# A two-layer hybrid encoder on one core: key blocks of the attention weights transposed two at a time instead of one at a time

## The chip, the core and the metric

The kernel runs on one NeuronCore of a Trainium2 chip, in a single launch. The metric is the device time of that launch in microseconds. A core has a matrix engine (TensorE, PE in the profile, with its weight loads as PEld), VectorE (DVE), ScalarE (ACT), GpSimd (POOL) and SyncE (SP, which here only issues transfers). Each engine works through its own list of instructions in order. They meet through semaphores, and the matrix engine writes only to PSUM, which DVE and ACT then read.

## The reference

Two layers, each with three attention branches side by side (MLA, a windowed GQA called SWA, and a differential attention), a gate on each, and an output product. The change touches the last step of two of the branches, the product of the attention weights with the values:

```python
# MLA, 8 heads, 512 tokens
p = jax.nn.softmax(s, axis=-1).astype(v.dtype)
return jnp.einsum('bhqk,bkhd->bqhd', p, v)
# differential attention, 4 heads
p = jax.nn.softmax(s, axis=-1)
a = p[:, 0] - lam * p[:, 1]
return jnp.einsum('bhqk,bkhe->bqhe', a.astype(v.dtype), v)
```

All is float32. The kernel holds accuracy by splitting a float32 operand in a rounded high part and the remainder, and multiplying high by high, low by high and high by low.

## The kernel before

Activations lie transposed, features on partitions and the 512 tokens along the free dimension. Large projections (`proj_T`, line 464) load a 128x1024 piece of weights into a tile `wr` (two buffers), ACT makes the high part `wh` (`act_copy`, L81), DVE the low part `wl` (`sub`, L84), and PE runs 24 products of 128x512 into a PSUM tile `ps_dn` (two buffers; `mm3`, lines 87 to 89).

An attention head has two steps. `first` makes the scores into `ps_sc` (two buffers), DVE takes the row maxima (L770), ACT the exponentials, and POOL scales the rows (L775), which leaves the weights `p` with queries on partitions. `second` needs keys on partitions. So for each block of 128 keys, `transposed_block` (line 701) takes a PSUM tile `ps_tr` (two buffers), has PE transpose four 128x128 pieces into it (L704), and copies it out in two parts: ACT writes the high part `pt` (L81), then DVE the low part, another `pt` (L84; `pt` has six buffers). Then PE multiplies both parts with the values into `ps_av` (one buffer): `av_step` in MLA (lines 713 to 717, two products a block), `mm3` in the differential attention (three a block). There are four blocks a head. After the last block the sum is read out of `ps_av` (L788 in MLA), and only then can the next head use that buffer.

`pipelined` (line 694) writes `first` of head h+1 before `second` of head h. SWA has a `second` of its own (line 898), which the change doesn't touch, but which uses the same `ps_tr`, `pt` and `ps_av`.

The written order is not the order on the engines. The kernel is handed to a scheduler, which goes through a model of the time, gives each tile a buffer when one is free, and puts each engine's instructions in the order in which they become ready there, with the written order as priority. So the loops mix: projections for later steps fill PE between the pieces of a head. `mod_late` (line 239) shares this stretch of layer 0: it loads pieces of `w_ada` into `wr` and sums them on DVE (L248, L251), and adds the result up through a `ps_dn` tile (L257, read by L261).

Of the kernel before, what the change touches and what calls it, by code (L numbers as in the profile page):

```python
# [17 lines left out]
P = 128  # L18
# [3 lines left out]
NT = S // P  # L22
# [28 lines left out]
def hybrid_kernel(ctx, tc, x, c, w_ada, b_ada, g_pre, g_post, w_in, g_q, w_uq, g_kv, w_ukv,  # L51
# [11 lines left out]
    def T(tag, shape, dt=F32, bufs=None):  # L63
        count[0] += 1
        return sb.tile(shape, dt, tag=tag, name=f"{tag}_{count[0]}",
                       bufs=bufs or BUFS.get(tag, 1))
# [6 lines left out]
    def Q(tag):  # L73
        count[0] += 1
        return ps.tile([P, S], F32, tag=tag, name=f"ps_{tag}_{count[0]}", bufs=PB[tag])

    def f(ap):
        return ap.bitcast(F32)

    def act_copy(out_, in_, scale=1.0):  # L80
        return act.activation(out=out_, in_=in_, func=AF.Copy, scale=scale)  # L81

    def sub(out_, a, b, eng=None):
        return (eng or dve).tensor_tensor(out=out_, in0=a, in1=b, op=ALU.subtract)  # L84

    def mm3(o, ah, al, bh, bl, start, stop):
        pe.matmul(o, ah, bh, start=start, stop=False)  # L87
        pe.matmul(o, ah, bl, start=False, stop=False)  # L88
        pe.matmul(o, al, bh, start=False, stop=stop)  # L89
# [392 lines left out]
    def split_u(o):  # L482
        uh = T("u", [P, S], F32R)
        ul = T("u", [P, S], F32R)
        act_copy(uh, o)
        sub(ul, o, f(uh))
        return uh, ul
# [213 lines left out]
    def transposed_block(blocks):  # L701
        tr = Q("tr")
        for i, b in enumerate(blocks):
            pe.transpose(tr[:, i * P:(i + 1) * P], b, ident)  # L704
        ph = T("pt", [P, S], F32R)
        pl = T("pt", [P, S], F32R)
        act_copy(ph, tr)
        sub(pl, tr, f(ph))
        return ph, pl

    def av_step(av, v, ph, pl, first, last):
        if not last:
            pe.matmul(av, v, ph, start=first, stop=False)  # L713
            pe.matmul(av[0:64], v[:, 0:64], pl, start=False, stop=False)  # L714
        else:
            pe.matmul(av[0:64], v[:, 0:64], pl, start=False, stop=False)
            pe.matmul(av, v, ph, start=False, stop=True)

    def mla_attention(l, cl, kp, v, wts):
# [59 lines left out]
        def second(h, pr):  # L779
            i = h % 2  # L780
            op = o_all[h // 2]
            av = Q("av")
            for kb in range(NT):
                ph, pl = transposed_block([pr[:, t, kb * P:(kb + 1) * P] for t in range(NT)])
                av_step(av, v[kb][:, h], ph, pl, kb == 0, kb == NT - 1)
            ol = T("ta", [P, S])
            act_copy(ol[0:64], av[64:128])
            dve.tensor_tensor(out=op[i * 64:(i + 1) * 64], in0=av[0:64], in1=ol[0:64], op=ALU.add)  # L788

        weights(0)  # L790
        prep(0)
        pipelined(first, second, 8)
        return o_all

# [142 lines left out]
    def diff_attention(l, hh, hl, fill):  # L937
# [31 lines left out]
        def second(hd, pr):  # L969
            vt = ops[hd][3]  # L970
            av = Q("av")
            for kb in range(NT):
                ph, pl = transposed_block([pr[:, t, kb * P:(kb + 1) * P] for t in range(NT)])
                vs = slice(kb * P, (kb + 1) * P)
                mm3(av, vt[:, 0, vs], vt[:, 1, vs], ph, pl, kb == 0, kb == NT - 1)
            sq = T("ta", [P, S])
            sqh = T("pt", [P, S], F32R)
            sql = T("pt", [P, S], F32R)
            act.activation(out=sq, in_=av, func=AF.Square)
            act_copy(sqh, sq)  # L980
            sub(sql, sq, f(sqh))
            sq_ps = Q("pj")
            pe.matmul(sq_ps, onesr, sqh, start=True, stop=False)
            pe.matmul(sq_ps, onesr, sql, start=False, stop=True)
            rs = T("ta", [P, S])
            act.activation(out=rs, in_=sq_ps, func=AF.Ln, scale=1.0 / P, bias=epsc)
            act.activation(out=rs, in_=rs, func=AF.Exp, scale=-0.5)
            o = T("o", [P, S])
            dve.scalar_tensor_tensor(out=o, in0=av, scalar=gsub[l], in1=rs, op0=ALU.mult,
                                     op1=ALU.mult)  # L990
            dve.tensor_tensor(out=o, in0=o, in1=zc[hd], op=ALU.mult)
            o_all.append(split_u(o))
# [4 lines left out]
        with tc.high_priority(offset=20):  # L997
            pr = first(0)
        for hd in range(4):
            zc[hd] = silu_z(l, C_ZC + hd * P, hh, hl)  # L1000
            fill(FN)
            if hd + 1 < 4:
                with tc.high_priority(offset=20):
                    nxt = first(hd + 1)
            with tc.high_priority(offset=20):
                second(hd, pr)
            pr = nxt
            if hd + 2 < 4:
                ops[hd + 2] = diff_qkv(l, hd + 2, hh, hl)
# [210 lines left out]
```

## Time and profile before

| | us |
|---|---|
| median of 3 runs | 1179.66 (1179.07 to 1180.35) |
| profiled execution, its own time | 1178.78 |
| its span | 1176.7 |
| PE busy | 1146.0 (97%) |
| DVE busy | 844.2 (72%) |
| ACT busy | 631.5 (54%) |

Read it so: the span is from the first to the last instruction of the program, the execution's own time has what lies around it, 2.1 us. A busy share is an average over the whole span, so the table says which engine is closest to its limit, and the rows further down say where it waits. Matmuls are pipelined, so the busy time of one (about 0.39 us) is longer than the step from one start to the next.

### The profile page before, as it was taken

To read this page: it belongs to the slowest core of one execution; us is meant where nothing else is said; L and a number is where in the kernel's file an instruction comes from. 1 tells how busy PE (TensorE), PEld (TensorE's weight loads), DVE (VectorE), ACT (ScalarE), POOL (GpSimd) and SP (SyncE) were. 2 spreads that over 40 slices of the span, in tenths; PEclk is the share of its full clock that TensorE was granted. 3 is DMA by queue.
4 is the path that set the end of the run, shared out by engine and by line. 5 is a ranking of instruction groups with operands and counts; after the bars stand their busy time and mean duration, and the time that the engine had idled before them with its cause. 6 is when DMAs were issued, how large, how long until landed. Compare 5 with 4: busy or idle time off the path is not lost.

```text
span 1176.7 us, 15536 instructions
## 1 busy us (share of the span) xinstructions
PE 1146.0 (97%) x5428; PEld 946.0 (80%) x5428; DVE 844.2 (72%) x1754; ACT 631.5 (54%) x1250; POOL 181.3 (15%) x226
## 2 busy tenths in 40 slices
PE   5899999999999999999999999999999999999997
PEld 4768788878887888888888888888888888888886
DVE  7956686898866687876577567688786568786654
ACT  5355464655543457664357456565564346675432
POOL 4310212122210010101211011222121001100120
PEclk9899999999999999999999999999999999999999
DMA  9537532256355433433454432324533333334442
GB/s 340 190 92 217 186 106 76 72 145 186 108 141 164 110 81 87 117 107 126 143 184 135 114 108 75 86 52 123 157 97 92 95 95 96 88 99 115 136 159 92
DMA packets 169522, 146.86 MB, mean 125 GB/s; under 512 B 7679, under 2 KB 146999, under 8 KB 169444
## 3 DMA queue, kind: packets, MB, share of 16 engines
q1 hardware_dynamic: 166148, 140.08, 40.9%
q10 hardware_dynamic: 3168, 5.77, 1.3%
q8 instruction: 43, 0.70, 0.2%
q14 instruction: 35, 0.29, 0.1%
q0 software_dynamic: 128, 0.01, 0.0%
HBM read 135.83 MB, written 14.20 MB: 127 GB/s over the span
## 4 chain that ended last, share of the span: by engine, by line
PE 84%; DVE 6%; DMA 3%; issue 3%; ACT 1%; POOL 1%; SPq 0%; DVEq 0%; POOLq 0%; ACTq 0%
PE ps_dn L87 20%; PE ps_dn L89 20%; PE ps_dn L88 19%; PE ps_tr L704 5%; PE ps_sc L89 2%; PE ps_sc L87 2%; PE ps_sc L88 2%; PE ps_av L714 1%; PE ps_av L713 1%; PE ps_sc L952 1%; PE ps_sc L953 1%; DMA wr<-in_w_in 1%; DVE o L206 1%; PE ps_pj L87 1%; PE ps_pj L88 1%
## 5 line engine op out<-in xcount | busy, mean ns | idle before, releaser
L87 PE MATMUL ps_dn<-hTh,wh 128*128 128x512 f32 x840 | 331.8, 395 | 1.4 <-DVE zz L479 0.8
L89 PE MATMUL ps_dn<-hTh,wl 128*128 128x512 f32 x840 | 330.5, 393 | 0.4 <-DVE wl L84 0.4
L88 PE MATMUL ps_dn<-hTl,wh 128*128 128x512 f32 x840 | 330.1, 393 | 0.0
L84 DVE TENSOR_TENSOR wl<-wr,wh 128x1024 fp32r<-128x1024 f32 x141 | 178.9, 1269 | 98.5 <-ACT wh L81 97.5
L81 ACT ACTIVATE wh<-wr 128x1024 fp32r<-128x1024 f32 x141 | 149.1, 1058 | 162.7 <-PE ps_dn L88 111.2
L87 PEld LDWEIGHTS ps_dn<-hTh,wh 128*128 128x128 f32 x840 | 158.2, 188 | 33.2 <-PE ps_dn L89 1.0
L89 PEld LDWEIGHTS ps_dn<-hTh,wl 128*128 128x128 f32 x840 | 158.0, 188 | 33.3 <-DVE wl L84 0.9
L88 PEld LDWEIGHTS ps_dn<-hTl,wh 128*128 128x128 f32 x840 | 158.1, 188 | 31.7
L84 DVE TENSOR_TENSOR pt<-ps_tr,pt 128x512 fp32r<-128x512 f32 x136 | 92.2, 684 | 30.5 <-ACT pt L81 29.6
L81 ACT ACTIVATE pt<-ps_tr 128x512 fp32r<-128x512 f32 x136 | 78.8, 596 | 64.8 <-PE ps_tr L704 63.6
L775 POOL TENSOR_SCALAR p<-p,st 128x512 f32<-128x512 f32 x64 | 52.2, 834 | 279.3 <-DVE st L773 243.7
L704 PE MATMUL ps_tr<-ident,p 128*128 128x128 f32 x544 | 92.4, 273 | 0.9 <-POOL p L775 0.6
L704 PEld LDWEIGHTS ps_tr<-ident,p 128*128 128x128 f32 x544 | 69.5, 141 | 20.2 <-POOL p L775 1.8
L87 PE MATMUL ps_dn<-u,wh 128*128 128x512 f32 x192 | 75.9, 395 | 0.0
L89 PE MATMUL ps_dn<-u,wl 128*128 128x512 f32 x192 | 75.9, 395 | 0.0
L88 PE MATMUL ps_dn<-u,wh 128*128 128x512 f32 x192 | 75.2, 391 | 0.0
L963 POOL TENSOR_SCALAR ta<-ta,st 128x512 f32<-128x512 f32 x32 | 26.7, 834 | 306.9 <-ACT wh L81 143.1
L894 POOL TENSOR_SCALAR p<-p,st 128x256 f32<-128x256 f32 (+1 forms) x64 | 42.1, 676 | 157.7 <-DVE st L892 130.4
L771 ACT ACTIVATE p<-ps_sc,st 128x512 f32<-128x512 f32 x64 | 43.7, 685 | 28.0 <-DVE st L770 27.7
L770 DVE TENSOR_REDUCE st<-ps_sc 128x1 f32<-128x512 f32 x64 | 43.4, 686 | 21.3 <-PE ps_sc L89 20.8
L886 ACT ACTIVATE p<-p,st 128x256 f32<-128x256 f32 (+1 forms) x64 | 35.7, 558 | 21.9 <-DVE st L884 21.2
L959 ACT ACTIVATE p<-p,st 128x512 f32<-128x512 f32 x32 | 23.1, 723 | 38.8 <-DVE st L957 38.7
(345 smaller groups left out, 2100.5 us busy)
## 6 DMA issues: line engine op xcount, KB each, us to landing
wr<-in_w_in SPq DMA_DIRECT2D x105, 512.0 KB, 3.7
wr<-in_w_ada SPq DMA_DIRECT2D x32, 512.0 KB, 3.6
wr<-in_w_out SPq DMA_DIRECT2D x16, 512.0 KB, 3.6
big<-in_w_ada SPq DMA_DIRECT2D x10, 512.0 KB, 7.6
big<-in_x SPq DMA_DIRECT2D x8, 512.0 KB, 5.3
wr<-in_w_o_mla SPq DMA_DIRECT2D x8, 512.0 KB, 4.0
wr<-in_w_o_swa SPq DMA_DIRECT2D x8, 512.0 KB, 3.4
wr<-in_w_o_diff SPq DMA_DIRECT2D x8, 512.0 KB, 3.7
```

The lines of the kernel that those rows point to most:

```text
L81: return act.activation(out=out_, in_=in_, func=AF.Copy, scale=scale)
L84: return (eng or dve).tensor_tensor(out=out_, in0=a, in1=b, op=ALU.subtract)
L87: pe.matmul(o, ah, bh, start=start, stop=False)
L88: pe.matmul(o, ah, bl, start=False, stop=False)
L89: pe.matmul(o, al, bh, start=False, stop=stop)
L704: pe.transpose(tr[:, i * P:(i + 1) * P], b, ident)
L770: dve.tensor_reduce(out=nm[:, t:t + 1], in_=s, axis=AX.X, op=ALU.max, negate=True)
L771: act.activation(out=pr[:, t], in_=s, func=AF.Exp, bias=nm[:, t:t + 1], accum_out=sm[:, t:t + 1])
L775: pool.tensor_scalar(out=pr[:, t], in0=pr[:, t], scalar1=rr[:, t:t + 1], scalar2=1.0, op0=ALU.mult, op1=ALU.mult)
L886: act.activation(out=pr[:, i, :w], in_=pr[:, i, :w], func=AF.Exp, bias=nm[:, i:i + 1], accum_out=sm[:, i:i + 1])
L894: pool.tensor_scalar(out=pr[:, i, :w], in0=pr[:, i, :w], scalar1=rr[:, i:i + 1], scalar2=1.0, op0=ALU.mult, op1=ALU.mult)
L963: pool.tensor_scalar(out=pc[1], in0=pc[1], scalar1=rr[:, 1:2], scalar2=1.0, op0=ALU.mult, op1=ALU.mult)
```

## The change

In both loops over the key blocks, the two blocks of a pair are now transposed and copied out in the written order before the products of either. No instruction is added or removed, and the products keep their order among themselves.

```diff
-            for kb in range(NT):
-                ph, pl = transposed_block([pr[:, t, kb * P:(kb + 1) * P] for t in range(NT)])
-                av_step(av, v[kb][:, h], ph, pl, kb == 0, kb == NT - 1)
+            for k0 in range(0, NT, 2):
+                pt = [transposed_block([pr[:, t, kb * P:(kb + 1) * P] for t in range(NT)])
+                      for kb in (k0, k0 + 1)]
+                for kb in (k0, k0 + 1):
+                    av_step(av, v[kb][:, h], *pt[kb - k0], kb == 0, kb == NT - 1)
```

The other loop, in the differential attention, is changed in the same way, with `mm3` in the place of `av_step`. Lines after the first loop stand two further down in the changed kernel (L788 becomes L790, L878 becomes L880), and names of tiles carry other numbers.

What the scheduler makes of it differs by place. In MLA of layer 1 no instruction moves on any engine. In the differential attention of either layer single transposes move by a few places. In layer 0, the lists start to differ in the fourth head of MLA and differ on through SWA, up to the first projections after it. In all, the transposes of L704 stand on PE in 196 uninterrupted rows before and in 188 now, of which rows of eight are 6 before and 11 now.

PE, layer 0, where the last MLA head's products start (`ps_av_1719`) beside the first scores of SWA (`ps_sc_25..`, L878). Before:

```order
L704 MATMUL ps_tr_1731<-ident_73,p_1638 128x128 x4
L257 MATMUL ps_dn_2440<-ones_78,u_2004 128x1 x4
L704 MATMUL ps_tr_1742<-ident_73,p_1638 128x128 x4
L878 MATMUL ps_sc_2515<-op_2202,op_2326 128x256
L879 MATMUL ps_sc_2515<-op_2203,op_2326 128x256
L878 MATMUL ps_sc_2535<-op_2202,op_2288 128x384
L879 MATMUL ps_sc_2535<-op_2203,op_2288 128x384
L713 MATMUL ps_av_1719<-pt_1725,big_866 128x512
L714 MATMUL ps_av_1719<-pt_1726,big_866 64x512
L713 MATMUL ps_av_1719<-pt_1736,big_873 128x512
L714 MATMUL ps_av_1719<-pt_1737,big_873 64x512
L704 MATMUL ps_tr_1753<-ident_73,p_1638 128x128 x4
```

The same place now (L880 is L878 of before, `pt_1734` and `pt_1735` are `pt_1736` and `pt_1737`):

```order
L880 MATMUL ps_sc_2515<-op_2202,op_2326 128x256
L881 MATMUL ps_sc_2515<-op_2203,op_2326 128x256
L257 MATMUL ps_dn_2440<-ones_78,u_2004 128x1 x4
L713 MATMUL ps_av_1719<-pt_1725,big_866 128x512
L714 MATMUL ps_av_1719<-pt_1726,big_866 64x512
L713 MATMUL ps_av_1719<-pt_1734,big_873 128x512
L704 MATMUL ps_tr_1742<-ident_73,p_1638 128x128 x4
L714 MATMUL ps_av_1719<-pt_1735,big_873 64x512
L704 MATMUL ps_tr_1751<-ident_73,p_1638 128x128 x4
L880 MATMUL ps_sc_2535<-op_2202,op_2288 128x384
L881 MATMUL ps_sc_2535<-op_2203,op_2288 128x384
L880 MATMUL ps_sc_2541<-op_2202,op_2289 128x384
```

The products into `ps_av_1719` moved ahead of the third block's transposes and of the second window's scores, and the first window's fourth score ahead of both.

DVE at the same place. Before (`ps_sc_2503` to `ps_sc_2515` are scores two to four of the first window, `o_1556` is the read-out of the head before):

```order
L248 TENSOR_SCALAR big_3119<-wr_3120,cact_66 128x512
L251 SCALAR_TENSOR_TENSOR big_3119<-wr_3120,cact_66,big_3119 128x512
L880 ISA p_2496,st_2491<-ps_sc_2503,x_548_2483,sinkt_72 128x256
L880 ISA st_2491 128x1
L880 ISA p_2496,st_2491<-ps_sc_2509,x_549_2486,sinkt_72 128x256
L880 ISA st_2491 128x1
L807 SCALAR_TENSOR_TENSOR op_2399<-ps_dn_2407,op_2399 64x512
L884 TENSOR_SCALAR st_2493<-st_2491 128x1
L788 TENSOR_TENSOR o_1556<-ps_av_1671,ta_1716 64x512
L884 TENSOR_SCALAR st_2493<-st_2491 128x1
L84 TENSOR_TENSOR pt_1737<-ps_tr_1731,pt_1736 128x512
L261 TENSOR_TENSOR ashf_8_70<-ps_dn_2440,prT_25_112 128x4
```

Now:

```order
L809 SCALAR_TENSOR_TENSOR op_2363<-ps_dn_2370,op_2363 64x512
L790 TENSOR_TENSOR o_1556<-ps_av_1671,ta_1716 64x512
L248 TENSOR_SCALAR big_3119<-wr_3120,cact_66 128x512
L84 TENSOR_TENSOR pt_1726<-ps_tr_1720,pt_1725 128x512
L84 TENSOR_TENSOR pt_1735<-ps_tr_1729,pt_1734 128x512
L251 SCALAR_TENSOR_TENSOR big_3119<-wr_3120,cact_66,big_3119 128x512
L882 ISA p_2496,st_2491<-ps_sc_2509,x_549_2486,sinkt_72 128x256
L882 ISA st_2491 128x1
L882 ISA p_2496,st_2491<-ps_sc_2515,x_549_2486,sinkt_72 128x256
L882 ISA st_2491 128x1
L809 SCALAR_TENSOR_TENSOR op_2399<-ps_dn_2407,op_2399 64x512
L261 TENSOR_TENSOR ashf_8_70<-ps_dn_2440,prT_25_112 128x4
```

The read-out of the head before and the two low parts `pt` of a pair stand together ahead of the scores of SWA, which they followed.

PE in SWA of layer 0, around one window's two transposed blocks (`ps_tr_2933`, `ps_tr_2944`) that no line of the diff touches. Before:

```order
L704 MATMUL ps_tr_2933<-ident_73,p_2832 128x128
L704 MATMUL ps_tr_2944<-ident_73,p_2832 128x128
L88 MATMUL ps_dn_3443<-hTl_121,wh_3438 128x512
L704 MATMUL ps_tr_2933<-ident_73,p_2832 128x128
L704 MATMUL ps_tr_2944<-ident_73,p_2832 128x128
L878 MATMUL ps_sc_2912<-op_2204,op_2399 128x384
L879 MATMUL ps_sc_2912<-op_2205,op_2399 128x384
L704 MATMUL ps_tr_2933<-ident_73,p_2832 128x128
L878 MATMUL ps_sc_2918<-op_2204,op_2400 128x384
L879 MATMUL ps_sc_2918<-op_2205,op_2400 128x384
L704 MATMUL ps_tr_2944<-ident_73,p_2832 128x128
L89 MATMUL ps_dn_3443<-hTh_120,wl_3439 128x512
```

Now, with the first products that use the blocks:

```order
L704 MATMUL ps_tr_2933<-ident_73,p_2832 128x128 x3
L704 MATMUL ps_tr_2944<-ident_73,p_2832 128x128
L704 MATMUL ps_tr_2933<-ident_73,p_2832 128x128
L704 MATMUL ps_tr_2944<-ident_73,p_2832 128x128 x3
L89 MATMUL ps_dn_3470<-u_2479,wl_3414 128x512
L257 MATMUL ps_dn_3484<-ones_78,big_3265 128x1 x4
L880 MATMUL ps_sc_2978<-op_2204,op_2362 128x256
L881 MATMUL ps_sc_2978<-op_2205,op_2362 128x256
L880 MATMUL ps_sc_2984<-op_2204,op_2363 128x256
L881 MATMUL ps_sc_2984<-op_2205,op_2363 128x256
L713 MATMUL ps_av_2932<-pt_2938,big_2245 128x512
L714 MATMUL ps_av_2932<-pt_2939,big_2245 64x512
```

The eight transposes moved into one row, behind two projections that they stood among, and nine products (one of 512 columns, four of one, four of 256) are left between them and the first product that needs them.

## Rows read from the trace of the kernel before

**Rows 1.** The page, part 1: busy us, share of the span, instructions.

```profile
PE 1146.0 (97%) x5428; PEld 946.0 (80%) x5428; DVE 844.2 (72%) x1754; ACT 631.5 (54%) x1250; POOL 181.3 (15%) x226
```

**Rows 2.** The page, part 4: the chain that ended last, by engine.

```profile
PE 84%; DVE 6%; DMA 3%; issue 3%; ACT 1%; POOL 1%; SPq 0%; DVEq 0%; POOLq 0%; ACTq 0%
```

**Rows 3.** Stretches: busy us of PE, PEld, DVE, ACT, POOL (instructions), granted clock, DMA.

```profile
190.00:245.00 55.00, 55.00 (x281) 44.79 (x280) 46.68 (x73) 32.16 (x64) 10.49 (x12) 1.00 0.30 87
245.00:253.00 8.00, 5.86 (x23) 4.23 (x23) 7.69 (x20) 4.57 (x11) 0.00 (x0) 0.79 0.58 138
253.00:380.00 127.00, 127.00 (x630) 105.83 (x630) 96.34 (x230) 63.19 (x132) 20.89 (x32) 1.00 0.52 147
...
700.00:870.00 170.00, 170.00 (x850) 139.85 (x849) 133.86 (x261) 102.28 (x216) 35.49 (x49) 1.00 0.35 98
```

**Rows 4.** Waits of PE, 125 to 1160 us: us in total, times, longest.

```profile
PE ps_sc L878 <- DVE st L880: 1.1, 1, 1.1
PE ps_av L713 <- DVE st L884: 0.9, 1, 0.9
PE ps_dn L87 <- DVE op L807: 0.6, 1, 0.6
PE ps_tr L704 <- POOL p L775: 0.6, 2, 0.3
```

**Rows 5.** Three short stretches, columns as in Rows 3.

```profile
140.00:150.00 10.00, 10.00 (x53) 8.23 (x52) 5.60 (x9) 4.83 (x12) 2.70 (x4) 1.00 0.27 80
245.00:249.00 4.00, 1.94 (x11) 1.19 (x10) 3.79 (x11) 1.01 (x3) 0.00 (x0) 1.00 0.81 177
249.00:253.00 4.00, 3.92 (x12) 3.03 (x13) 3.91 (x11) 3.57 (x9) 0.00 (x0) 0.57 0.36 99
```

**Rows 6.** PE in order of time: start us, busy us, line, tiles, [idle before].

```profile
149.32 1.03 PE L704 MATMUL ps_tr<-ident,p 128*128 128x128 f32 x8
150.11 0.48 PE L88 MATMUL ps_dn<-hTl,wh 128*128 128x512 f32 x1
150.42 0.40 PE L89 MATMUL ps_dn<-hTh,wl 128*128 128x512 f32 x1
150.65 0.39 PE L87 MATMUL ps_dn<-hTh,wh 128*128 128x512 f32 x1
...
157.01 0.60 PE L704 MATMUL ps_tr<-ident,p 128*128 128x128 f32 x4
157.37 0.48 PE L713 MATMUL ps_av<-pt,big 128*128 128x512 f32 x1
157.69 0.39 PE L89 MATMUL ps_dn<-hTh,wl 128*128 128x512 f32 x1
```

**Rows 7.** DVE in order of time, layer 0, end of MLA.

```profile
243.40 1.23 DVE L84 TENSOR_TENSOR wl<-wr,wh 128x1024 fp32r<-128x1024 f32 x1
...
247.57 0.68 DVE L807 SCALAR_TENSOR_TENSOR op<-ps_dn,op 64x512 fp32r<-64x512 f32 x1
...
248.36 0.67 DVE L788 TENSOR_TENSOR o<-ps_av,ta 64x512 f32<-64x512 f32 x1
...
249.61 0.14 DVE L261 TENSOR_TENSOR ashf<-ps_dn,prT 128x4 f32<-128x4 f32 x1
```

**Rows 8.** PE in order of time, the same place.

```profile
247.19 0.39 PE L878 MATMUL ps_sc<-op,op 128*128 128x256 f32 x1 [1.13 <-DVE st L880]
...
249.08 0.61 PE L713 MATMUL ps_av<-pt,big 128*128 128x512 f32 x1 [0.87 <-DVE st L884]
...
251.48 0.78 PE L87 MATMUL ps_dn<-hTh,wh 128*128 128x512 f32 x1
...
252.84 0.40 PE L87 MATMUL ps_dn<-hTh,wh 128*128 128x512 f32 x1
```

**Rows 9.** Instructions on `ps_tr`: ns min/median/max, first and last start us.

```profile
L81 ACT ACTIVATE pt<-ps_tr x136: 576/598/608, 133.6 to 1082.8; 128x512 fp32r<-128x512 f32 x136
L84 DVE TENSOR_TENSOR pt<-ps_tr,pt x136: 658/684/694, 134.2 to 1083.5; 128x512 fp32r<-128x512 f32 x136
```

**Rows 10.** The page, part 6: KB each, median us from issue to landing.

```profile
wr<-in_w_ada SPq DMA_DIRECT2D x32, 512.0 KB, 3.6
```

More of the change, by code (lines that the diff above doesn't have):

```diff
@@ L971, in second @@
             av = Q("av")
[L972 to L975, printed above, removed]
+            for k0 in range(0, NT, 2):
+                pt = [transposed_block([pr[:, t, kb * P:(kb + 1) * P] for t in range(NT)])
+                      for kb in (k0, k0 + 1)]
+                for kb in (k0, k0 + 1):
+                    vs = slice(kb * P, (kb + 1) * P)
+                    mm3(av, vt[:, 0, vs], vt[:, 1, vs], *pt[kb - k0], kb == 0, kb == NT - 1)
             sq = T("ta", [P, S])
```

## The prediction

> **What bounds the kernel now.** I read the page first. PE is busy 97% of the span [rows 1] and 84% of the chain that ended last is PE [rows 2]. So PE is the engine to beat, and a change that leaves its instructions as they are can only win or lose what PE spends waiting, or running slowly. Next I read where PE waits between 125 and 1160 us: four waits, 3.2 us in all [rows 4]. The stretches say where the first two lie: in 245 to 253 us PE is busy for 5.86 of 8 us and its granted clock is 0.79, while before and after it is busy all the time at 1.00 [rows 3]. In that stretch DVE is busy 7.69 of 8 us, and in the 55 us ahead 46.7 [rows 3]: there PE waits for a DVE that has fallen behind. [...] So the place costs 8 - 5.86 = 2.1 us of waiting and 4 x 0.43 = 1.7 us of low clock, 3.8 us. It is inside the part of the program that the change reorders. In MLA of layer 1 (700 to 870 us) PE has no idle time at all [rows 3], and there the lists are the same.
>
> **The change, part by part.** It adds and removes nothing; the work that hides each moved step is the projections around it.
>
> *The rows of transposes.* A row of eight and the product behind it take 150.42 - 149.32 = 1.10 us; a row of four and its product 157.69 - 157.01 = 0.68 [rows 6]. With a step of 0.23 from product to product (150.65 - 150.42) [rows 6], eight transposes cost 0.87 us and two rows of four 2 x 0.45 = 0.90. A merged pair saves 0.03 us. There are 188 rows instead of 196, so 8 x 0.03 = 0.2 us at most; I take 0.2, with 0 as the other end.
>
> *The eviction.* A pair in a row needs both `ps_tr` buffers, and the third block needs the first one back, after ACT's 0.60 and DVE's 0.68 us [rows 9]. That is 1.3 us, and no wait of PE for it shows before: the transposes' own waits are 0.6 us, for POOL [rows 4]. I price it at nothing in MLA, where projections fill PE between pairs; without them it would be 1.3 - 0.87 = 0.4 us a pair.
>
> *The stretch at 245 us.* Here the order decides. Before, PE waits for DVE to read a score and give back `ps_sc` (until 247.19), then for the read-out of `ps_av` (named L884 in the row; the buffer's reader is L788, which ends at 248.36 + 0.67 = 249.03), and it goes on at 249.08 [rows 7, 8]. The next projection starts at 251.48, its fourth product at 252.84 [rows 8]. Now the fourth score stands ahead, L788 and the low parts of the pair precede the scores on DVE, and the projection follows L261, which gives its `ps_dn` back. I place L261 by differences from its start of 249.61 [rows 7]: one more score ahead of it, +0.5; two small L884 behind it, -0.2; one eviction earlier in the list that goes into idle time of DVE before 245 us (8.3 us of it [rows 3]), -0.6; and a wait for a weight piece, because the sum that frees its `wr` stands later: transfer 3.6 us [rows 10] and its copy on ACT bring the part `wl` 0 to 1 us later than DVE gets there, I take 0.9. That makes 250.2. The projection then starts at about 250.4 instead of 251.48, 1.1 us earlier, with two products of 384 columns already done (2 x 0.17, from 0.23 for 512). If the clock stays up, its first three products take 0.7 instead of 1.36 us. Sum: 1.1 + 0.3 + 0.7 = 2.1 us gained. If the clock falls in the same place, half of the 2.3 us from 250.4 to 252.7 is lost again: 1.0 us gained. PE's waits there are not fewer, only spread: for a `ps_dn` before L257, for L788, for the first low part, for L261, 2 to 3 us against 2.0. A single wait of 0.6 us at another place [rows 4] left the clock at 1.00. I take the middle, 1.5 us, and keep 0 and 2.1 as ends.
>
> *SWA behind it.* Its lists move because the scheduler starts it in another state. PE has no wait there before (127.00 of 127 us busy [rows 3]). The third table of PE shows the tightest place now: after the first block's last transpose PE has 0.3 us of transposes and nine products, about 1.4 us, then L713 of 0.23, before it needs the low part `pt_2939`. ACT and DVE need 1.3 us for that if both are free [rows 9]; but on DVE two scores of 0.5 us and a weight piece of 1.23 us [rows 7] now stand ahead of it, which makes about 2.5 us. So PE waits 2.5 - 1.7 = 0.8 us if the weight piece is there, and 0 if DVE is ahead; above, 1.2 us, a whole piece more than free. I take 0.8. Weights are not late: of the waits of PE [rows 4] none is for a weight piece, and the queue of SP keeps its order, but for one bias table.
>
> *The rest.* The differential attention moves single transposes by a few places, which costs or saves 0.03 us each, nothing. No part lies under the wait of 0.6 us for L807 [rows 4]; it stays.
>
> Sum: -0.2 - 1.5 + 0.8 = -0.9 us. Against the execution of 1178.78 us that gives 1177.9; the median of the runs lies 0.9 above that execution, so 1178.8.
>
> [...] The rows show that a row of eight transposes does not slow PE by itself: 140 to 150 us holds one and has a clock of 1.00 [rows 5]. [...]
>
> **The rivals.** *The stretch opens up (faster).* The early read-out of `ps_av` and the early low parts take the wait away, and with it the low clock. For it: both named waits of the place are for instructions that now stand earlier on DVE. Against it: DVE is busy all the time there and has the same work up to L261. Price: up to 2.1 + 1.7 + 0.2 = 4.0 us without a new wait in SWA, 1175.7; with half of the waiting left 3.0, 1176.7. It decides once DVE reaches L261 before about 249.
>
> *The clock falls a second time (slower).* In SWA the row of eight, four one-column products and the wait for `pt_2939` stand together, and PE goes on at half clock: 1.7 us [rows 5] and the wait of up to 1.2 us. It ends above the bound if the stretch at 245 gains nothing either (three waits where there were two): +2.9 - 0.2 = +2.7, 1182.4. For it: the same mix preceded the fall at 249 us. Against it: the wait there was 2.1 us, more than twice this one.
>
> *It does nothing.* The written order is only a priority; layer 1's MLA is the same list, and the products of before mostly stood behind the next block's transposes already. Then 1179.7.
>
> **How the numbers follow.** A measurement of this kernel can tell about 0.2%, 2.4 us, from no change. Forecast, a net between -2.4 and +2.4 us with the place at 245 us shifted: 0.48; nothing: 0.20; opened up: 0.20; second fall: 0.12. So faster 0.20, same 0.68, slower 0.12. The range leaves out about one in ten at either end. Its low end, 1176.4, lies between the faster rival with half of the waiting left (1176.7) and with none (1175.7); its high end, 1181.9, holds the forecast's dearest ends (no gain at 245 us, 1.2 us in SWA: 1180.9) and stops short of the slower rival's 1182.4.
>
> **What would show it.** Right: PE's busy time unchanged within 1 us; 245 to 253 us still the worst stretch, with waits named for DVE (L261 or L809, L790 and L84); the first projection after MLA starting about 1 us earlier; a wait of under 1.2 us for a low part `pt` in SWA near 327 us; the trace from 400 us on the same as before but shifted. Wrong: no low clock near 250 us (the faster rival), a second stretch with a clock under 1.00 near 327 us (the slower), or waits in the differential attention or in layer 1, which I cost at nothing.

## The result and the profile after

The changed kernel is a little slower: 1182.53 us median of 9 runs (1181.56 to 1185.99) against 1180.17 (1178.28 to 1181.35) for the kernel before on the same chip, ratio 1.0027 with a 95% interval of 1.0018 to 1.0036. That is about 3.2 us, between 2.1 and 4.2; the ratio compares all runs of the two and isn't the quotient of the medians, which lie 2.4 us apart. The forecast was 1178.8 us and "no difference". It started from three runs of the kernel before with a median of 1179.66, 0.5 us under the 1180.17 of nine.

The page of the changed kernel, parts 1 and 4, against [rows 1, 2]:

```profile
PE 1147.0 (97%) x5428; PEld 946.3 (80%) x5428; DVE 843.5 (71%) x1754; ACT 631.1 (53%) x1250; POOL 178.8 (15%) x226
...
PE 77%; DVE 9%; DMA 6%; issue 3%; ACT 2%; POOL 1%; SPq 1%; DVEq 0%; POOLq 0%; ACTq 0%
```

The work is the same to within 1 us on PE. The chain that ended last has less of PE and more of DVE and of transfers (6% DMA instead of 3%), but these shares don't go with the time: in e7 below, which is nearly as fast as the kernel before, PE has 75% and DMA 7%, and in e4, which is as slow as the changed kernel, 87% and 2%. The stretches say more, against [rows 3] (columns as there; this execution runs 1.9 us later than the one of before already at 184 us, where no list differs yet):

```profile
190.00:245.00 55.00, 54.94 (x275) 44.23 (x274) 47.08 (x75) 29.16 (x59) 11.36 (x15) 1.00 0.30 86
245.00:253.00 8.00, 6.06 (x35) 4.53 (x33) 6.76 (x16) 5.54 (x12) 0.00 (x0) 1.00 0.56 141
253.00:380.00 127.00, 123.57 (x609) 102.31 (x610) 95.24 (x233) 63.53 (x135) 18.27 (x32) 1.00 0.52 146
700.00:870.00 170.00, 170.00 (x849) 139.93 (x848) 131.39 (x254) 101.04 (x215) 36.57 (x48) 1.00 0.36 102
```

At 245 us the clock stays at 1.00, and the place costs 1.9 us instead of 3.8. Behind it, in the sliding-window attention (SWA), PE was busy all of 127 us before and is now idle for 127 - 123.57 = 3.4 us. Layer 1 is untouched. The waits of PE from 125 to 1160 us, against [rows 4] (line numbers behind the change are 2 to 4 higher):

```profile
PE ps_av L714 <- DVE pt L84: 1.7, 2, 0.9
PE ps_dn L257 <- DVE op L809: 1.0, 1, 1.0
PE ps_sc L880 <- DVE st L882: 1.0, 1, 1.0
PE ps_dn L87 <- DVE zz L479: 1.0, 1, 1.0
PE ps_tr L704 <- POOL p L775: 0.6, 2, 0.3
PE ps_sc L87 <- ACT p L771: 0.6, 1, 0.6
PE ps_dn L87 <- DVE op L809: 0.5, 1, 0.5
PE ps_av L713 <- ACT pt L81: 0.4, 1, 0.4
PE ps_dn L87 <- DVE ashf L261: 0.3, 1, 0.3
```

L257, one of the two of L714, and L261 are the place at 245 us. The wait for L771 lies at 130 us, where no list differs, and the one for L809 at L87 is the 0.6 us for L807 of before, at 386 us. Three places are new and lie in SWA: L880 at 260 us, L87 for `zz` at 285 us, and L713 with the other L714 at 333 us. On SP only two bias tables stand later; they are issued from 339 us on, behind all three. The third place is the clearest. ACT, DVE and PE in order of time there:

```profile
331.92 1.06 ACT L81 ACTIVATE wh<-wr 128x1024 fp32r<-128x1024 f32 x1 [2.18 <-DMA wr<-in_w_in]
332.88 0.58 ACT L81 ACTIVATE pt<-ps_tr 128x512 fp32r<-128x512 f32 x1
...
333.01 1.23 DVE L84 TENSOR_TENSOR wl<-wr,wh 128x1024 fp32r<-128x1024 f32 x1 [1.10 <-ACT wh L81]
...
334.22 0.68 DVE L84 TENSOR_TENSOR pt<-ps_tr,pt 128x512 fp32r<-128x512 f32 x1
...
333.51 0.50 PE L713 MATMUL ps_av<-pt,big 128*128 128x512 f32 x1 [0.42 <-ACT pt L81]
334.96 0.45 PE L714 MATMUL ps_av<-pt,big 128*64 128x512 f32 x1 [0.95 <-DVE pt L84]
```

Read it from PE backwards. L714 waits for a low part `pt`, which stands on DVE behind the low part `wl` of a weight piece. DVE had nothing to do for 1.10 us before that `wl`, because ACT's `wh` waited 2.18 us for the transfer. So one late transfer holds ACT and DVE, and what PE needs is queued behind it on both. In the kernel before, DVE's list has the same pieces in another order:

```
# before
L84 TENSOR_TENSOR pt_2939<-ps_tr_2933,pt_2938 128x512
...
L84 TENSOR_TENSOR wl_3530<-wr_3528,wh_3529 128x1024
...
L84 TENSOR_TENSOR wl_3554<-wr_3552,wh_3553 128x1024
# after
L84 TENSOR_TENSOR wl_3530<-wr_3528,wh_3529 128x1024
...
L84 TENSOR_TENSOR wl_3554<-wr_3552,wh_3553 128x1024
...
L84 TENSOR_TENSOR pt_2939<-ps_tr_2933,pt_2938 128x512
```

(lines between are left out), and in the trace of before the three stand so (DVE in order of time):

```profile
322.89 0.68 DVE L84 TENSOR_TENSOR pt<-ps_tr,pt 128x512 fp32r<-128x512 f32 x1
...
326.84 1.23 DVE L84 TENSOR_TENSOR wl<-wr,wh 128x1024 fp32r<-128x1024 f32 x1 [0.97 <-ACT wh L81]
...
333.35 1.22 DVE L84 TENSOR_TENSOR wl<-wr,wh 128x1024 fp32r<-128x1024 f32 x1
```

DVE waited for weights there too (0.97 us), but nothing that PE needed soon stood behind it. Over 185 to 385 us DVE's waits for weight pieces have hardly grown; first the row of before, then of after (us in total, times, longest):

```profile
DVE wl L84 <- ACT wh L81: 15.1, 11, 4.0
```

```profile
DVE wl L84 <- ACT wh L81: 16.8, 12, 3.4
```

ACT's waits for the transfer itself grew more, again first before, then after:

```profile
ACT wh L81 <- DMA wr<-in_w_in: 13.5, 8, 4.4
```

```profile
ACT wh L81 <- DMA wr<-in_w_in: 23.4, 8, 5.3
```

Such a sum doesn't say what is lost, though, as e5 and e6 will show; what stands behind the wait does.

The wait at 260 us has the same form. PE made the scores of a block at 252 us. DVE then stood idle before a `wl`, and reduced the scores only after it, so PE got its `ps_sc` back late:

```profile
251.78 0.44 PE L880 MATMUL ps_sc<-op,op 128*128 128x384 f32 x1
...
259.37 1.23 DVE L84 TENSOR_TENSOR wl<-wr,wh 128x1024 fp32r<-128x1024 f32 x1 [1.41 <-ACT wh L81]
...
260.82 0.62 DVE L882 CUSTOM_DVE_ANT_0 p<-ps_sc,x,sinkt 128x384 f32<-128x384 f32 x1
...
261.50 0.44 PE L880 MATMUL ps_sc<-op,op 128*128 128x384 f32 x1 [1.01 <-DVE st L882]
```

DVE idles for 1.41 us though the scores of that reduction have been complete since 252.8 us: in DVE's list the reduction stands behind the `wl`, and it started only after that, at 260.82 us.

The wait at 285 us has no late transfer just ahead of it. ACT's half of `zz` stands behind exponentials (L888) that waited 1.81 and 0.55 us for DVE, and DVE, which works without a gap from 279.24 us on, comes late to its own half:

```profile
283.37 0.62 ACT L888 ACTIVATE p<-p,st 128x384 f32<-128x384 f32 x1 [1.81 <-DVE st L886]
...
285.24 0.58 ACT L478 ACTIVATE zz<-ps_dn 128x512 f32<-128x512 f32 x1
...
285.95 0.68 DVE L479 SCALAR_TENSOR_TENSOR zz<-zz,ps_dn 128x512 f32<-128x512 f32 x1
...
286.69 0.50 PE L87 MATMUL ps_dn<-hTh,wh 128*128 128x512 f32 x1 [0.96 <-DVE zz L479]
```

### The profile page after: what moved, and what is told of

It reads as the page before. It is cut to its first block, busy times and chain, and to the rows that moved or that the text cites. A ratio compares the mean times of both kernels' runs of the same rounds, so it can differ in the third digit from the quotient of the medians.

```text
span 1181.8 us, 15529 instructions
## 1 busy us (share of the span) xinstructions
PE 1147.0 (97%) x5428; PEld 946.3 (80%) x5428; DVE 843.5 (71%) x1754; ACT 631.1 (53%) x1250; POOL 178.8 (15%) x226
## 4 chain that ended last, share of the span: by engine, by line
PE 77%; DVE 9%; DMA 6%; issue 3%; ACT 2%; POOL 1%; SPq 1%; DVEq 0%; POOLq 0%; ACTq 0%
PE ps_dn L87 18%; PE ps_dn L89 18%; PE ps_dn L88 18%; PE ps_tr L704 4%; DMA wr<-in_w_in 3%; DVE wl L84 2%; PE ps_sc L89 2%; PE ps_sc L87 2%; PE ps_sc L88 2%; DMA wr<-in_w_ada 2%; PE ps_sc L954 1%; PE ps_sc L955 1%; PE ps_av L714 1%; PE ps_av L713 1%; DMA big<-in_x 1%
## 5 line engine op out<-in xcount | busy, mean ns | idle before, releaser
L87 PE MATMUL ps_dn<-hTh,wh 128*128 128x512 f32 x840 | 331.8, 395 | 2.1 <-DVE zz L479 1.2
L87 PEld LDWEIGHTS ps_dn<-hTh,wh 128*128 128x128 f32 x840 | 157.9, 188 | 35.1 <-DVE zz L479 1.8
L84 DVE TENSOR_TENSOR pt<-ps_tr,pt 128x512 fp32r<-128x512 f32 x136 | 91.8, 684 | 34.1 <-ACT pt L81 33.3
L704 PE MATMUL ps_tr<-ident,p 128*128 128x128 f32 x544 | 90.5, 272 | 0.8 <-POOL p L775 0.6
L704 PEld LDWEIGHTS ps_tr<-ident,p 128*128 128x128 f32 x544 | 68.7, 140 | 19.1 <-POOL p L775 1.5
L87 PE MATMUL ps_dn<-u,wh 128*128 128x512 f32 x192 | 76.1, 397 | 0.0
L896 POOL TENSOR_SCALAR p<-p,st 128x256 f32<-128x256 f32 (+1 forms) x64 | 39.5, 635 | 168.3 <-DVE st L894 124.1
L771 ACT ACTIVATE p<-ps_sc,st 128x512 f32<-128x512 f32 x64 | 43.7, 685 | 29.5 <-DVE st L770 28.9
L888 ACT ACTIVATE p<-p,st 128x256 f32<-128x256 f32 (+1 forms) x64 | 35.6, 557 | 34.4 <-DVE st L886 33.6
```

The lines of the kernel that those rows point to most:

```text
L771: act.activation(out=pr[:, t], in_=s, func=AF.Exp, bias=nm[:, t:t + 1], accum_out=sm[:, t:t + 1])
L888: act.activation(out=pr[:, i, :w], in_=pr[:, i, :w], func=AF.Exp, bias=nm[:, i:i + 1], accum_out=sm[:, i:i + 1])
L896: pool.tensor_scalar(out=pr[:, i, :w], in0=pr[:, i, :w], scalar1=rr[:, i:i + 1], scalar2=1.0, op0=ALU.mult, op1=ALU.mult)
```

## The experiments

**Theory A**: the price is the new order of the lists in SWA of layer 0, wherever it comes from. **Theory B**: the differential attention's moved transposes cost it. **Theory C**: it is the pairs themselves, in the MLA heads. **Theory S**: the order in the MLA heads lets the weight transfers fall behind before 245 us, and the splits come late in any order. To compare traces I number PE's matmuls (transposes and one-column products included) by their start, from 0; number 755 starts at 182 to 186 us, number 1215 near 280, number 1600 at 353 to 360. Both stretches hold equally many products of each width in the two kernels. The time between such numbers leaves out what differs between executions ahead of the change. All ratios are to the kernel before on the same chip. In the texts of the expectations a tile has its number in the code: `pt_675` is the `pt_2939` above, `wl_800` the `wl_3554`.

| run | ratio (95% interval) | matmul 755 to 1215, us | 1215 to 1600, us |
|---|---|---|---|
| kernel before | 1 | 95.76 | 75.13 |
| changed kernel | 1.0027 (1.0018 to 1.0036) | 95.73 | 78.20 |
| e1 MLA pairs alone | 1.0026 (1.0016 to 1.0037) | 95.07 | 78.05 |
| e2 differential pairs alone | 1.0004 (0.9995 to 1.0013) | 95.28 | 75.13 |
| e3 head 3 alone | 1.0006 (0.9997 to 1.0015) | 94.64 | 75.13 |
| e4 head 4 alone | 1.0025 (1.0015 to 1.0035) | 95.96 | 76.20 |
| e5 heads after, SWA before | 0.9993 (0.9984 to 1.0002) | 95.74 | 75.09 |
| e6 heads before, SWA after | 1.0018 (1.0010 to 1.0027) | 93.90 | 79.04 |
| e7 after, one split later | 1.0006 (0.9997 to 1.0014) | 94.78 | 76.45 |
| e8 before, scores first | 0.9999 (0.9990 to 1.0009) | 95.18 | 75.10 |
| e9 after, `wl_715` later | 0.9996 (0.9988 to 1.0005) | 95.29 | 75.19 |
| e10 after, place cleared | 1.0016 (1.0007 to 1.0024) | 94.47 | 76.53 |
| e11 half transfers | 1.0009 (1.0000 to 1.0018) | 93.34 | 81.24 |
| e12 fewer products on DVE | 0.9993 (0.9984 to 1.0002) | 94.66 | 76.30 |

### One half of the change at a time

e1 has the first hunk of the diff, e2 the second.

> Pairs written in the latent heads' second alone (both layers), the differential attention as before. Every engine's list is then the changed kernel's up to the end of layer 0's sliding-window attention and the kernel before's after it. Theory A (layer 0's sliding-window attention, whose DVE list now holds weight splits earlier, loses about 4.2 us of TensorE time in three waits, and the place at 245 us gains 1.3): as slow as the changed kernel, ratio 1.002 to 1.003, time 1182 to 1183 us, with TensorE waits of about 1 us each near 260, 285 and 333 us. Theory B (the moved transposes of the differential attention cost the time, and the waits near 260 to 333 us belong to that one execution): 1180.2 us, ratio 1.000.

> Pairs written in the differential attention's second alone. Lists differ from the kernel before's only in 44 places of TensorE's, from 412 us on, and 4 of DVE's and ACT's. Theory A: 1180.2 us, ratio 1.000, and the start offset of TensorE's rows against the kernel before stays within 0.5 us over that stretch. Theory B: 1182 to 1183 us, ratio 1.002 to 1.003.

e1 gives the whole loss, e2 nothing that can be measured. B falls. e1's profile repeats the three waits in SWA (0.9 us for the score, 0.9 for `zz`, 0.3 and 0.9 for the two `pt`), so they were no accident of one execution; that the first two aren't in every execution, e7 shows.

### One head at a time

With the pairs in a single head the scheduler moves other lists by itself. Of layer 0's eight heads (counted from 0) only pairs in head 3 and in head 4 change any list at all, and layer 1's change none.

```diff
-            for kb in range(NT):
-                ph, pl = transposed_block([pr[:, t, kb * P:(kb + 1) * P] for t in range(NT)])
-                av_step(av, v[kb][:, h], ph, pl, kb == 0, kb == NT - 1)
+            for k0 in range(0, NT, (2 if l == 0 and h == 3 else 1)):
+                kbs = range(k0, k0 + (2 if l == 0 and h == 3 else 1))
+                pt = [transposed_block([pr[:, t, kb * P:(kb + 1) * P] for t in range(NT)])
+                      for kb in kbs]
+                for kb in kbs:
+                    av_step(av, v[kb][:, h], *pt[kb - k0], kb == 0, kb == NT - 1)
```

> Pairs in layer 0's latent head 3 alone. The lists differ from the kernel before's only from 190 to 260 us; the whole of the sliding-window attention behind 260 us has the order of before. Theory A: no wait behind 260 us that before lacks; the place at 245 us keeps between 0 and 1.3 us of gain: 1178.9 to 1180.2 us, ratio 0.999 to 1.000. Theory C (the price is that of the pairs themselves in the latent heads, in their PSUM buffers and evictions, and grows with the reordered rows): a part of the 2.4 us by the share of moved places (218 of 591), 1181 us, ratio 1.0008.

> Pairs in layer 0's latent head 4 alone. Lists differ from 205 to 348 us: 424 places of TensorE's, and in the sliding-window attention some weight splits stand up to 11 places earlier on DVE (17 in the changed kernel), others later. Theory A: the loss goes with how early the splits stand against the data that they wait for, so between before and after: 1180.5 to 1182 us, ratio 1.0003 to 1.0015, with its waits in the sliding-window attention. Theory C: by the share of moved places (424 of 591) 1181.9 us, ratio 1.0014, its waits at head 4's rows, from 205 to 230 us.

e3 leaves SWA's lists behind 260 us as they were, and the second stretch takes 75.13 us as before. Its ratio doesn't decide: the interval, 0.9997 to 1.0015, holds C's 1.0008 as well as A's 1.000. e4 changes the lists, and pays more than either theory gave it, 1.0025 instead of up to 1.0015 and 1.0014. Its trace shows only part of these 2.9 us: from matmul 755 to 1600 it takes 172.15 us against 170.89 in the kernel before, with PE idle for 83 - 82.19 = 0.8 us from 277 to 360 us, in one wait for `zz`. The rest stays open.

```profile
277.00:360.00 83.00, 82.19 (x421) 68.31 (x420) 63.58 (x167) 41.43 (x93) 14.17 (x24) 1.00 0.47 141
```

C would have put e4's waits at head 4's rows, from 205 to 230 us; there is none there. But a single head is still a pair, so these two don't refute C alone.

### The heads of one kernel with the SWA of the other

Here a rule for the scheduler queues one DVE instruction behind another one. Such a rule moves the state in which the scheduler enters SWA, and two of them happen to give the crossed cases: e5 has the changed kernel's lists to 257 us and the order of before from 280 us on; e6 has no pairs, and the changed kernel's lists from 286 us on, but for a few single transposes up to 289 us.

```diff
# e5, on the changed kernel (rec holds the reductions by tile and row)
+    pin = {729: [('p', 567, 1)]}
-                sub(lw[:, :n], raw[:, :n], f(h[:, :n]))
+                with behind(*[rec[x] for x in pin[nl]]) if nl in pin else nullcontext():
+                    sub(lw[:, :n], raw[:, :n], f(h[:, :n]))
# e6, on the kernel before, around the first product of mod_late
+    mpin = {(719, 0): ("p", 557, 2)}
+                    with behind(rec[mpin[nr, 0]]) if (nr, 0) in mpin else nullcontext():
```

> The changed kernel with one more rule for the scheduler: on DVE the split wl_729 of layer 0 is queued behind the second reduction of the sliding-window block p_567. With it DVE's list goes back to the order of before: TensorE's list is the changed kernel's up to row 1094 (about 257 us) and the kernel before's from row 1204 (about 280 us) to the end of layer 0. So: the latent heads of after, the sliding-window order of before. Theory A (the changed order in the sliding-window attention costs the time, whatever leads to it): the stretch of TensorE's rows 1215 to 1600 takes 75.1 us again as before (78.0 to 78.2 in the changed kernel), and the gain of the place at 245 us shows: ratio 0.9988 to 1.0003. Theory S (the order in the latent heads lets the stream of weight transfers fall behind by 1.2 us before 245 us, and the splits come late in any order): waits of about 1 us stay behind 260 us: ratio 1.0015 to 1.0030.

> The kernel before, no pairs anywhere, with one rule for the scheduler: on DVE the first read of the transfer wr_719 is queued behind the third reduction of the sliding-window block p_557. That moves two reductions ahead at 245 us, and from TensorE's row 1237 (about 286 us) to the end of layer 0 every list is the changed kernel's. So: the latent heads of before, the sliding-window order of after. Theory A: slow as the changed kernel though nothing is paired, the stretch of rows 1215 to 1600 takes 77 to 78.2 us, ratio 1.0010 to 1.0030. Theory S: the stream of transfers is as early as before, no wait: ratio 0.9985 to 1.0003.

From 190 to 277 and from 277 to 360 us, e5:

```profile
190.00:277.00 87.00, 85.08 (x420) 69.38 (x420) 75.13 (x142) 49.39 (x101) 15.61 (x21) 0.98 0.38 110
277.00:360.00 83.00, 83.00 (x424) 69.14 (x423) 64.17 (x168) 42.93 (x94) 16.27 (x24) 1.00 0.48 146
```

and e6:

```profile
190.00:277.00 87.00, 85.21 (x431) 69.55 (x429) 74.51 (x143) 50.81 (x103) 15.06 (x20) 1.00 0.36 108
277.00:360.00 83.00, 81.52 (x404) 67.22 (x403) 60.45 (x159) 40.83 (x90) 13.73 (x24) 0.98 0.48 145
```

e5 pairs every head and has PE busy all of the second stretch; e6 pairs none, and PE idles there for 1.5 us and loses another 0.02 x 83 = 1.7 us to the clock, which puts its second stretch (79.04 us) above the forecast 77 to 78.2. The slow half of the cross goes with SWA's order, not with the pairs: C falls. S falls too: e5 keeps the changed order in the heads, and the time is that of before. Its ACT waits for transfers nearly as long as the changed kernel's, and e6's less than before; from 185 to 385 us, e5 and then e6:

```profile
ACT wh L81 <- DMA wr<-in_w_in: 19.6, 8, 5.0
```

```profile
ACT wh L81 <- DMA wr<-in_w_in: 12.7, 6, 4.0
```

So late transfers alone don't cost the time. What the slow lists have in common is where weight splits stand on DVE. In the changed kernel and in e6, `wl_774` and `wl_800` stand 17 places earlier than before, in e4 `wl_800` stands 11 places earlier; in e5 no split stands more than one place earlier, in e9 (below) none more than four. It isn't all: e10 is slow without it, and e7 keeps most of it and is nearly as fast as the kernel before (both below).

### One of the waits taken away

e7 is the changed kernel with the split `wl_800` behind `pt_678` (`pin = {800: [('pt', 678)]}`), so that it no longer stands ahead of `pt_675`.

> The changed kernel, where DVE's split wl_800 is queued behind the low part pt_678 instead of ahead of pt_675; lists differ from the changed kernel's only from 333 us to the end of layer 0. Both theories: TensorE's waits at 333 us for pt_674 and pt_675 (0.42 and 0.95 us, 1.8 us with the clock and the pipeline) go, ratio 1.0008 to 1.0015 in place of 1.0026. If the wait only moves to the product that needs wl_800: still 1.0020 to 1.0030.

PE and DVE at that place:

```profile
330.46 0.50 PE L718 MATMUL ps_av<-pt,big 128*128 128x512 f32 x1 [0.39 <-ACT pt L81]
...
330.44 0.69 DVE L84 TENSOR_TENSOR pt<-ps_tr,pt 128x512 fp32r<-128x512 f32 x1 [0.87 <-ACT pt L81]
```

The wait for DVE is gone and the one for ACT, forecast to go too, stays (0.39 us), since ACT's high part of that weight piece still stands ahead. The ratio falls from 1.0027 and 1.0026 to 1.0006, by 2.4 us and just under the forecast 1.0008. The stretch from matmul 1430 to 1600 says how much of that is this place: 1.2 us (33.8 us against 35.0). The rest of its trace's gain is the execution's, since e7's lists equal the changed kernel's up to 333 us: its waits at 260 and 285 us are 0 and 0.3 us instead of 1.0 and 1.0. So one instruction moved on DVE behind two low parts takes back 1.2 us; where the other 1.2 us between the ratios come from isn't shown, and the two intervals are wide enough to hold a good part of them.

### Is there something to gain at 245 us?

e8 is the kernel before with two rules there (`pin = {715: [("p", 557, 1)]}`, `mpin = {(719, 0): ("p", 557, 2)}`). e9 is the changed kernel with `pin = {715: [("q", 522), ("pt", 419)]}` (`q` is a low part of `stack_q`), e10 has `mpin = {(719, 0): ("pt", 422)}` in addition (and e5's rule for `wl_729`, which with these two changes no list). **Theory W**: each wait is a matter of the few rows ahead of it. **Theory G**: DVE and the transfers that it frees carry the time up to 280 us, and a PE wait taken away comes back.

> The kernel before, no pairs, with two rules on DVE at 245 us: the split wl_715 behind the second reduction of block p_557, the first read of wr_719 behind its third. The reductions for which TensorE waits there (1.1 and 0.9 us, with the low clock 3.3 us in all) then come first. The order behind it shifts in 250 of TensorE's rows, up to 349 us, no split of weights far ahead. Theory A: the place gives back 1.5 to 3 us and the sliding-window attention keeps most of it: ratio 0.9975 to 0.9990. Theory S says the same of the place, but the splits queued later hold the transfers back by 0.5 us: 0.9985 to 1.0005.

> The changed kernel with one rule at 245 us: on DVE the split wl_715 stands behind the low parts op_522 and pt_419, for which TensorE waits there (1.0 and 0.7 us). The sliding-window lists are then those of before from TensorE's row 1380 (about 310 us) on, so the wait at 333 us should be absent. Theory W (each wait is a matter of the few rows ahead of it): the stretch of TensorE's rows 755 to 1215 falls from 95.1 to 95.7 us by 1.5 to 2 us, and the ratio to the kernel before is 0.9975 to 0.9988. Theory G (up to 280 us DVE and the weight transfers that it frees carry the time; a TensorE wait taken away at 245 us comes back by 285 us): rows 755 to 1215 stay within 94.6 to 96 us, ratio 0.9990 to 1.0005.

> As the run before, and in addition the first read of the transfer wr_719 stands behind the low part pt_422: at 245 us everything on DVE for which TensorE waits there comes ahead of the work for the weights. Theory W: rows 755 to 1215 fall by 2 to 3 us, ratio 0.9970 to 0.9985. Theory G: TensorE's waits only come later, near 260 and 285 us, rows 755 to 1215 within 94.6 to 96 us, ratio 0.9990 to 1.0008.

In the first stretch (755 to 1215) none of them gets below 94.4 us, against 95.3 and 95.8 for the order of before (e2 has that order too). e8 misses the 1.5 to 3 us that A and S both expected of the place; its ratio lies in S's range and above A's, though its SWA costs nothing (75.10 us). Its waits only changed places, 1.3 and 0.7 us instead of 1.1 and 0.9, and the clock fell as before (0.87 from 245 to 249 us, 0.70 from 249 to 253).

W's numbers don't come, and G's hold for e9 and just fail for e10 (94.47 us for 94.6). But G's reason, that the waits come back, isn't what e9 and e10 show. PE's waits from matmul 755 to 1215 add up to 3.0 us in the changed kernel, to 1.5 in e9 and to 0.8 in e10, so they went by about what W said. The clock took the gain: it is 1.00 at 245 to 253 us in the changed kernel's trace and 0.79 in these two, 8 x 0.21 = 1.7 us. e6, whose one rule is one of e8's two, kept the clock there and took 93.90 us, less than G's 94.6. The stretch in e6, e9 and e10:

```profile
245.00:253.00 8.00, 6.25 (x31) 4.59 (x32) 7.84 (x21) 4.81 (x11) 0.00 (x0) 1.00 0.59 164
```

```profile
245.00:253.00 8.00, 6.88 (x29) 5.14 (x29) 7.46 (x18) 4.10 (x7) 0.00 (x0) 0.79 0.45 132
```

```profile
245.00:253.00 8.00, 7.03 (x33) 5.58 (x32) 7.02 (x16) 5.17 (x12) 0.00 (x0) 0.79 0.43 126
```

For G speaks one comparison: the changed kernel, e1 and e7 have the same lists up to 333 us. The first two kept the clock at 249 us (1.00 to 253 us) and waited 0.9 to 1.0 us at 260 us and again at 285; e7 lost it (0.58) and waited 0 and 0.3. So W against G stays open: one trace of each doesn't say how often the clock falls.

e9's SWA is that of before and so is its time. e10's ratio of 1.0016 fits neither theory, and its one trace, with 0.7 us of new idle time from 277 to 360 us, doesn't account for the 1.9 us; that stays open.

### Transfers or DVE's work?

G names two carriers. e11 halves the late modulation's transfers, e12 takes half of its products off DVE.

```diff
# e11
-                sp.dma_start(out=raw, in_=w_ada[l]... [:, k:k + 2, q * S:(q + 1) * S])
+                sp.dma_start(out=raw[:, 0], in_=w_ada[l]... [:, k, q * S:(q + 1) * S])
# e12
-                for i in range(k == 0, 2):
+                for i in range(k == 0, 1):
```

> The kernel before, but each transfer of the late modulation rows brings one row of two (256 KB instead of 512 KB) and that row is read twice: layer 1's modulation is then wrong, DVE's work is the same. The scheduler's lists shift (782 of TensorE's rows, up to 349 us). If the transfers themselves bound the stretch from 190 to 285 us, TensorE's rows 755 to 1215 lose most of the 4.0 us of waits and low clock: 92 to 93.5 us, ratio 0.9965 to 0.9980. If DVE's queue does, 94.5 to 96 us, ratio 0.9990 to 1.0010.

> The kernel before without the second product of each transfer of the late modulation rows: 16 products of 0.74 us less on DVE (10 or 11 of them between 216 and 288 us, about 8 us), transfers unchanged; layer 1's modulation is then wrong. The scheduler's lists shift (615 of TensorE's rows, up to 282 us). If DVE's queue bounds the stretch, TensorE's rows 755 to 1215 take 91.8 to 93.5 us, ratio 0.9960 to 0.9980. If the transfers do, 94.5 to 96 us, ratio 0.9990 to 1.0010.

Neither makes the kernel measurably faster. e11 gains 2 us in the first stretch and loses 6 in the second, in one wait of 2.7 us for `zz` and a low clock behind it (0.90 from 285 to 320 us). e12 has 7 us less on DVE from 190 to 277 us (67.90 us busy against 74.88 before):

```profile
190.00:277.00 87.00, 84.91 (x424) 69.73 (x423) 67.90 (x136) 49.39 (x102) 14.98 (x20) 0.98 0.42 125
277.00:360.00 83.00, 82.51 (x416) 68.18 (x415) 59.40 (x156) 41.82 (x91) 16.15 (x24) 1.00 0.43 130
```

PE still waits: 87 - 84.91 = 2.1 us, and 1.9 of it in one wait for L261. So less of DVE's work hardly shortens the stretch (94.66 us, where 91.8 to 93.5 was forecast if DVE's queue bounds it). Of the bytes the two runs don't decide: e11's first stretch (93.34 us) is what was forecast if the transfers bound it, its ratio is what was forecast if they don't, and 1.7 of the 2.4 us that it gains there are the clock, which stayed at 1.00, as it did in e6 with whole transfers. Both also change the lists, from about 111 us on, so they don't say what less work would do under a fixed order. What is left, argued and not shown, is the order: each list has its own place where DVE waits for a transfer, or is busy with something that can wait, while PE needs what stands behind.

No version beats both kernels measurably. e5 and e9 keep the pairs and are 3.7 to 4.0 us ahead of the changed kernel (0.9993 and 0.9996 against 1.0027), but not apart from the kernel before.

## Why the prediction was wrong, step by step

*What bounds the kernel.* PE bounds it, and in the part that the change reorders only the place at 245 us had a loss: right as far as it went. It read the waits of PE alone. The row that would have warned, DVE's 15.1 us of waiting for weight pieces from 185 to 385 us, was in the trace of before. Its size doesn't tell a slow list from a fast one (16.8 us in the changed kernel, 16.0 in e5), but it says that DVE stands before late weights, and that whatever is moved behind them waits too.

*Rows of transposes, evictions, the rest.* Right where a run can tell: layer 1's MLA keeps PE busy for 170.00 of 170 us, no wait in MLA names an eviction outside the place at 245 us, and the differential attention costs nothing that can be measured (e2). No run shows the 0.2 us of the merged rows by themselves.

*The stretch at 245 us, -1.5.* Part of the mechanism came as told: the waits are spread (L257 1.0, L714 0.7, L261 0.3, the forecast's "2 to 3 us against 2.0"), and the clock stays up, at 1.00 where it was 0.79. The low clock that the forecast priced, 4 x 0.43 us, comes from the 0.57 of [rows 5]: 1 - 0.57 = 0.43. By itself the place gained 3.8 - 1.9 = 1.9 us. But DVE came later than forecast: with the 1.9 us taken off by which this execution is late already at 184 us, L261 starts at 252.88 - 1.9 = 251.0 instead of 250.2, and the first projection at 253.09 - 1.9 = 251.2, 0.3 us earlier than before instead of 1.1:

```profile
252.88 0.16 DVE L261 TENSOR_TENSOR ashf<-ps_dn,prT 128x4 f32<-128x4 f32 x1
...
253.09 0.50 PE L87 MATMUL ps_dn<-hTh,wh 128*128 128x512 f32 x1 [0.29 <-DVE ashf L261]
```

PE then gave 1.0 us back at 260 us; in e7, where the clock fell with the same rows, there was nothing to give back. Over matmuls 755 to 1215 the changed order took 95.73, 95.07 and 94.78 us (changed kernel, e1, e7), that of before 95.76 and 95.28: a gain of 0.3 us where 1.5 was forecast, inside its ends, and the wait at 260 us was costed at nothing.

*SWA, +0.8.* This is the step that failed. The forecast named the low part `pt_2939` behind a weight piece, and the wait is there: 0.95 us, within its 0 to 1.2. It made three errors around it. It took the piece to be there in time, and ACT waited 2.18 us for its transfer; "Weights are not late" was read from PE's waits, and it is ACT and DVE that wait for weights. ACT's list was left out: 0.42 us more for the high part. And one place was costed where three had changed: `zz` at 285 us adds 1.0. Together, over matmuls 1215 to 1600, SWA lost 78.1 - 75.1 = 3.0 us where 0.8 was forecast. 2.1 to 2.3 us of that are the waits named; for the rest no row gives a name.

From matmul 755 to 1600 the changed order took 173.93 and 173.12 us (changed kernel and e1) and that of before 170.89 and 170.41 (kernel before and e2), 2.7 to 3.0 us more, within the measured 2.1 to 4.2. So the sum was off by 2.2 us in SWA and by 1.2 us at 245 us. SWA's error alone would have made it +1.3 us, still "no difference"; it took both terms.

*The rivals.* The slower case was held at 0.12, with a second fall of the clock as its cause. The clock stayed at 1.00 from 253 to 380 us in the changed kernel, so the slowdown was that rival's and the mechanism was not. The sign of the faster rival came as well, no low clock near 250 us, and the kernel got no faster. What the slower rival called half clock is 0.50, from 250 to 252 us in the kernel before. The second fall was not far-fetched: in e6, where the same two waits are 0.2 and 0.95 us, the clock falls behind them:

```profile
332.00:336.00 4.00, 4.00 (x14) 3.18 (x13) 2.45 (x12) 1.54 (x5) 2.28 (x4) 0.72 0.78 212
```

What was missing was the plain rival, that SWA's order itself gets worse at several places. It needs no clock, and with the forecast's own upper price of 1.2 us at three places it comes to an estimate of 3.6 us.

## What to carry to other kernels

When a change lets a scheduler redo a stretch, the stretches behind it are part of the change, even where their code is untouched: compare their lists for instructions that wait for a transfer and now stand ahead of something that the busiest engine needs. Read the waits of every engine, not only those of the bottleneck; a wait that costs nothing today shows where a new order can cost. And follow a gain to the next place where the engines meet: here two executions that kept the clock at 249 us waited 0.9 to 1.0 us longer for DVE at 260 us than one of the same lists that lost it.

## What was not expected of the hardware

The granted clock fell, or not, for the same rows. The changed kernel, e5 and e7 have the same PE list at 245 to 253 us, with waits there of 1.02 and 0.72 us, 0.77 and 0.70, 0.76 and 0.47. Yet from 249 to 253 us the changed kernel's row is

```profile
249.00:253.00 4.00, 3.08 (x16) 1.99 (x16) 3.94 (x10) 1.61 (x4) 0.00 (x0) 1.00 0.55 132
```

that of e5

```profile
249.00:253.00 4.00, 4.00 (x17) 3.65 (x16) 3.94 (x12) 2.65 (x5) 0.00 (x0) 0.57 0.44 143
```

and that of e7

```profile
249.00:253.00 4.00, 4.00 (x15) 3.52 (x14) 3.90 (x12) 3.16 (x7) 0.00 (x0) 0.58 0.42 137
```

The shorter waits had the low clock, 0.57 and 0.58. e1 and e10 have the same PE list there too (e10 up to 252 us): e1 waits 0.89 and 0.46 us and stays at 1.00, e10 waits 0.20 and 0.57 and falls. One long wait doesn't decide it either: e3 waits 2.1 us at once and stays at 1.00, e4 2.0 us and falls. First e3, then e4:

```profile
249.00:253.00 4.00, 4.00 (x20) 3.20 (x21) 3.94 (x11) 2.36 (x4) 0.00 (x0) 1.00 0.40 133
```

```profile
249.00:253.00 4.00, 3.27 (x11) 2.27 (x12) 3.94 (x10) 2.17 (x5) 0.00 (x0) 0.62 0.45 134
```

What decides is open; in e5 the fall cost 1.7 us (4 x 0.43), so it is worth keeping as two outcomes in a forecast, as this one did for its place. The two rows of four transposes (L704, L708 in e5) stood at full clock in the changed kernel, 0.60 us each, and took 1.05 us each in e5: such rows alone don't bring the fall.
